# Job end times of the side work, POOL's DMA queue for the gate stores, and a third product from the old raw buffer

## The chip, the core and the metric

The kernel runs on one core of a Trainium2 chip. A core has five engines that each work through their own queue in a fixed order: PE (matrix products, results in PSUM), DVE (elementwise), ACT (elementwise, activation functions), POOL (elementwise, and it can issue DMAs), SP (issues DMAs only). They meet through semaphores. The metric is the device time of one execution in microseconds (us); the number compared is the median over several executions.

## What is computed

One layer of a decoder with 1024 prompt rows and 8 decode rows (1032 rows by 2048 columns). Cut to what matters:

```python
h = rmsnorm(x)
(aq, ak, av, iq, ik, iw, az, mq, mk, mv, mi, mf, mo, mz) = split(h @ w_in)
att = sparse_attend(top 256 keys of an index score)         # prompt; decode rows over a paged cache
h_ml, C, n, m = mlstm_run(mq, mk, mv, ig, lf)               # chunks, state C carried from chunk to chunk
a   = att * silu(az)
mo_ = rmsnorm_per_head(h_ml) * ml_norm_w * sigmoid(mo) * silu(mz)
x   = x + concat([a, mo_]) @ w_out
y   = rmsnorm(x)
```

The outputs are y for prompt and decode rows, the new keys and values and index keys, and the mLSTM states.

## The kernel before, in words

**The products.** Every fp32 operand of a large product is kept as a rounded high part H and a remainder L (`xH`, `xL`, `wH`, `wL`), and a product is the sum of three matmuls, H by H, H by L, L by H. Weights come by DMA into a raw fp32 buffer, ACT casts them to H, DVE subtracts to get L.

**Tiles.** The input projection is written as tiles numbered 0 to 60, and this number is also the clock by which side work is planned. Tiles up to 36 are plain (`mm`, L1500; `vproj`, L1569): T_MV = 9, T_AK = 17, T_AQ = 21, T_MQ = 29, T_MK = 33. From T_G = 37 to 60 comes the gate stage (`gate_stage`, matmuls L1729): the 24 tiles of the gates mo, mz and az as 12 pairs, each pair as 7 products of sums (kinds 0 to 4, 6, 7) in place of 8. That is 84 products of 48 matmuls with 258 columns, 4032 matmuls; after each half of a product `tick` is called, 168 "units" in all, each counted as one seventh of a tile. The products run in this order: kinds 4 and 6 together (units 0 to 47), kind 1 (to 71), kind 3 (to 95), kind 2 (to 119), and kinds 0 and 7 together (120 to 167). The sums of X rows that they multiply with are made early by the job `prep` (L1389 and around, DVE, ACT, POOL) and kept in DRAM as `xsD`; the sums of weights by the job `usum` (POOL DMAs that accumulate, L1419).

After the gate stage comes the output product for the last 264 rows (L1995, weights by `wsplit`, L248 to L252), then the tall product for the other 768 rows (L2056).

**Side work.** Attention, index scores, mLSTM and the preparations are written as generators ("jobs") in three lanes. A lane takes its jobs one after the other; at each tick `Lane.step` runs the current job until its share of work is done. The share follows from the job's weight and from the tile at which it is planned to end:

```python
quarters = max(1.0, self.job.end * 4 - self.now)
cost = w * quarters / max(self.left, w)
```

So a job's end sets how thickly its steps are written between the products. Lane 0 holds gates, index, att (prompt attention) and ml (prompt mLSTM); lane 1 prep, dscore, dsel, datt and dml (decode); lane 2 usum. What is written down this way is then given to a scheduler which fixes the order of every engine at build time; it can move an instruction forward or back, but not past what it depends on, and a buffer of a pool goes to its users in the order in which they were written.

**Prompt mLSTM.** `job_ml` has 16 steps, 8 chunks by 2 pairs of heads. One step is two transposes and two products for the scores (L853, L855), splits on ACT and DVE (`split`, L825 on ACT, L826 on DVE), then for each of two heads the matmuls of the output (L892) and of the state update (L896), then DVE, ACT and POOL, then transposes (L926). The products with qH, qL need the state C that an earlier step left, and buffers `dH`, `qH`, `CH`, `ksH` exist once each.

**PSUM.** The pool behind `bank()` has five banks; attention, mLSTM and decode jobs share them. The plain tiles and the gate stage have three more, `pj`. The last loop of the gate stage (kinds 0 and 7) needs four banks, so it takes one from `bank()`: `both = (pj[:2], [pj[2], bank()[:, :CS]])`. This bank can first be written when its earlier owners, written before unit 120, have been read.

**Gate weights.** `wide` (L1711 DMA, L1712 ACT cast, L1713 DVE) fetches the weights of a product into a raw buffer. The first products use the old raw buffer of the plain tiles (`one`, of which there is one: `wraw`); at a certain turn of the counter `turn["n"]` the rings of the plain tiles' wH and wL are turned into raw buffers, which the plain tiles must have left by then.

**Gate values.** In the last phases `gate_mz` and `gate_az` make two tanh operations on ACT, then two multiplications on POOL (`times`, L1790 and L1791 for az), then store 128 by 516 values to `gateS` in DRAM (L1782, L1792). The store was kept in the list `after` and issued on SP one product later. When the store of row k has been issued, `ready` gets k, and from tile T_PRE on `tick` issues `mixload` (L1468 the gate row from `gateS`, L1472 the attention or mLSTM row), and two ticks or more later `mixmake` (DVE L1477 and L1478, ACT, DVE), for the 14 rows of `PRE`; before the first of these the jobs ml and dml are run to their end.

Of the kernel before, what the change touches and what calls it, by code (L numbers as in the profile page):

```python
# [54 lines left out]
T_PRE = 58  # L55
# [115 lines left out]
def body(tc, A, stop=None):  # L171
# [1264 lines left out]
    def ix_weight(blocks):  # L1436
# [8 lines left out]
                   Job("att", T_MQ, 46.75, 2 * 2 * sum(2 * (1 + (i + 1) * 0.5) for i in range(8)) + 14, job_att, att_free),  # L1445
                   Job("ml", T_G + 9, T_PRE - 0.5, 38, job_ml)]),
             Lane([Job("prep", 4, T_AK, 8 * 16, job_prep),
                   Job("dscore", T_AK, 23, 24 + 128 + 2, job_dscore),
# [6 lines left out]
    after = []  # L1455
# [180 lines left out]
    def gate_stage():  # L1636
# [62 lines left out]
        def wide(kind, i):  # L1699
            turn["n"] += 1  # L1700
            if turn["n"] == 3:
                H, L = (wst.plain(name) for name in ("wH", "wL"))
                mlc["bc"] = raws[0][:2]
                raws[:] = [[x[:, 0], x[:, 1], x[:, 0:2]] for x in (H, L)] + [[H[:, 2], L[:, 2], None]]
                turn["raw"] = 0
# [69 lines left out]
        def gate_mz(j, h, e, g):  # L1775
            s2 = ev()
            half_tanh(s2, e)

            def times():
                G.tensor_tensor(s2, s2, e, OP.mult)  # L1780
                G.tensor_tensor(s2, s2, g, OP.mult)
            return times, lambda: SY.dma_start(row(8 + j)[:, cut(h)], flat(s2))  # L1782

        def gate_az(j, h, e, g):
# [7 lines left out]
            return times, lambda: SY.dma_start(row(j)[:, cut(h)], flat(s2))  # L1792

        def gate_raw(j):
            e, g = (take("s2", free).rearrange("p (c t) -> p c t", c=2) for _ in range(2))
            SY.dma_start(flat(e), row(j)[:, cut(0)])
            SY.dma_start(flat(g), rcS[j // 4][j % 4, :HR].partition_broadcast(128))
            push(*gate_az(j, 0, e, g))
# [66 lines left out]
        for i in range(NP):  # L1865
# [4 lines left out]
            with tc.high_priority():  # L1870
                for f in gate(i, 0, 1, combine(ps, got.pop(0), OP.add), g) or ():
                    f()
# [19 lines left out]
        def push(times, store, ks=()):  # L1892
            muls.append(times)
            after.append(lambda: (store(), ready.extend(ks)))

        def flush(n=1):
            while muls:
                muls.pop(0)()
            while len(after) > n:
                after.pop(0)()  # L1900

        for p, (z, i, y) in enumerate(order):
# [3 lines left out]
            with tc.high_priority():  # L1906
                fs = gate(i, 1, 1 - z, combine(both[y], e, OP.subtract, ev() if p > 1 else e), g)
            ks = () if z else [8 + i] if i < NM else [k for k in (2 * (i - NM), 2 * (i - NM) + 1) if k in PRE]
            push(*fs, ks)
# [17 lines left out]
    for f in after:  # L1927
        f()
# [436 lines left out]
```

## Time and profile before

| | |
|---|---|
| median of 3 executions | 2066.09 us (2060.03 to 2069.18) |
| the profiled execution, its own time | 2060.7 us |
| its span in the profile | 2058.6 us, 36195 instructions |
| mean granted clock of PE | 0.979 |
| PE busy | 1951.6 us, 12710 matmuls |
| DVE, ACT, POOL busy | 1436.4, 939.4, 417.0 us |
| DMA | 442.46 MB |
| gate stage | its first matmul starts at 946.4 us, its last at 1703.9 |
| mLSTM steps on PE | from 1421.3 to 1627.4 us |
| output product | its first matmul starts at 1704.0 us |

The profiled execution is one of its own; 2.1 us of its time lie outside the span. In the rows, L is a line of the kernel; "PEclk" is the granted clock of PE as a share of full speed; in a row of the timeline the bracket at the end gives how long the engine was idle before this instruction and what it waited for, "bank L892 <- ACT qH L825" in the waits means that matmuls of L892 into a tile named bank waited for ACT writing qH at L825.

### The profile page before, as it was taken

What the parts mean: (1) busy time and instruction counts of PE and PEld (TensorE: products, weight loads), DVE (VectorE), ACT (ScalarE), POOL (GpSimd) and SP (SyncE); (2) the same over time, 40 slices, a digit from 0 to 9 for tenths busy, and PEclk for the clock granted to TensorE, in tenths of its full rate; (3) what the DMA queues carried; (4) which work ended last, traced back from release to release, by engine and by line L of the source; (5) the groups of instructions that cost most, each with busy time, mean ns of one, the idle gap of its engine ahead of it and who ended that gap; (6) DMA issues with size and microseconds to landing.
All of it is one profiled execution on the core that took longest, in us unless ns stands there. A gap on an engine that the chain in (4) does not pass through costs nothing. (4 is left out here: it accounts for less than half of the span.)

```text
span 2058.6 us, 36195 instructions
## 1 busy us (share of the span) xinstructions
PE 1951.6 (95%) x12710; PEld 1841.5 (89%) x12710; DVE 1436.4 (70%) x3234; ACT 939.4 (46%) x1952; POOL 417.0 (20%) x420
## 2 busy tenths in 40 slices
PE   9988899999999999998999999999959998999997
PEld 9987788899999999998989999999959998986886
DVE  8454678976766677786835556666867575789886
ACT  8133455455313335321324555555656544455554
POOL 0111111213321010102210000000525452106542
PEclk9999999999999999999999999999979999999999
DMA  7567656667877587638645658677957877898875
GB/s 251 141 178 233 202 174 188 186 212 233 223 216 181 146 210 200 164 87 286 211 148 190 222 175 277 188 244 248 320 173 221 204 228 241 270 339 273 283 247 183
DMA packets 279603, 442.46 MB, mean 215 GB/s; under 512 B 41253, under 2 KB 142949, under 8 KB 275581
## 3 DMA queue, kind: packets, MB, share of 16 engines
q1 hardware_dynamic: 270189, 400.63, 61.0%
q0 software_dynamic: 7936, 37.76, 8.3%
q8 instruction: 100, 1.64, 0.3%
q10 hardware_dynamic: 1296, 1.77, 0.2%
q14 instruction: 82, 0.67, 0.1%
HBM read 344.33 MB, written 146.05 MB: 238 GB/s over the span
## 5 line engine op out<-in xcount | busy, mean ns | idle before, releaser
L1500 PE MATMUL pj<-xH,wH 128*128 128x344 f32 (+1 forms) x1200 | 389.3, 327 | 9.5 <-DVE iqe L377 5.1
L1500 PE MATMUL pj<-xL,wH 128*128 128x344 f32 (+1 forms) x1200 | 389.7, 325 | 0.0
L1500 PE MATMUL pj<-xH,wL 128*128 128x344 f32 (+1 forms) x1200 | 388.5, 324 | 0.0
L1729 PE MATMUL pj<-xH 128*128 128x258 f32 x1152 | 331.3, 288 | 9.6 <-DVE ev L1814 4.8
L1729 PE MATMUL pj<-xH,xL 128*128 128x258 f32 x1152 | 330.2, 287 | 2.5 <-DVE xL L1713 2.5
L1729 PE MATMUL pj<-xL,xH 128*128 128x258 f32 x1152 | 329.2, 286 | 0.9 <-issue 0.8
L1500 PEld LDWEIGHTS pj<-xH,wH 128*128 128x128 f32 x1200 | 226.6, 189 | 12.7 <-DVE iqe L377 6.1
L1729 PEld LDWEIGHTS pj<-xH 128*128 128x128 f32 x1152 | 220.0, 191 | 11.7 <-issue 4.6
L1500 PEld LDWEIGHTS pj<-xL,wH 128*128 128x128 f32 x1200 | 226.6, 189 | 1.3 <-DVE xL L309 0.3
L1500 PEld LDWEIGHTS pj<-xH,wL 128*128 128x128 f32 x1200 | 226.8, 189 | 0.9
L1729 PEld LDWEIGHTS pj<-xH,xL 128*128 128x128 f32 x1152 | 220.0, 191 | 5.2 <-DVE xL L1713 2.8
L1729 PEld LDWEIGHTS pj<-xL,xH 128*128 128x128 f32 x1152 | 220.2, 191 | 3.3 <-issue 2.3
L251 ACT CAST wH<-wraw 128x512 fp32r<-128x512 f32 (+2 forms) x183 | 109.7, 609 | 236.0 <-PE pj L1500 163.3
L252 DVE TENSOR_TENSOR wL<-wraw,wH 128x512 fp32r<-128x512 f32 (+2 forms) x183 | 129.7, 720 | 88.4 <-ACT wH L251 86.3
L2056 PE MATMUL pj<-wH,sH 128*128 128x512 f32 x336 | 132.4, 395 | 1.0 <-ACT wH L2040 0.8
L538 ACT ACTIVATE eq<-eq 128x512 bf16<-128x512 bf16 (+2 forms) x93 | 78.5, 844 | 117.1 <-DVE eq L537 107.8
L2056 PE MATMUL pj<-wH,sL 128*128 128x512 f32 x336 | 131.9, 393 | 0.0
L2056 PE MATMUL pj<-wL,sH 128*128 128x512 f32 x336 | 126.2, 394 | 4.0 <-DVE wL L2045 3.8
L491 ACT ACTIVATE rl<-bank 128x512 f32<-128x512 f32 (+2 forms) x160 | 79.8, 524 | 81.4 <-PE bank L489 47.3
L494 DVE SCALAR_TENSOR_TENSOR s<-rl,wiN,s 128x512 f32<-128x512 f32 (+2 forms) x150 | 98.8, 684 | 14.3 <-ACT rl L491 11.3
L489 PE MATMUL bank<-ki,qi 128*128 128x512 f32 (+2 forms) x320 | 79.1, 366 | 11.0 <-DMA qi<-qS 5.6
L882 POOL CAST aH<-onec 128x4 fp32r<-128x4 f32 x16 | 5.0, 314 | 375.0 <-DMA ev<-spD 375.0
(499 smaller groups left out, 4768.8 us busy)
## 6 DMA issues: line engine op xcount, KB each, us to landing
wraw<-in_wt_dram SPq DMA_DIRECT2D x144, 256.0 KB
wraw<-in_wa_dram SPq DMA_DIRECT2D x110, 256.0 KB
usD<-in_wa_dram POOLq DMA_DIRECT2D x48, 512.0 KB
xsD<-hl SPq DMA_DIRECT2D x80, 258.0 KB
wraw<-in_wo_dram SPq DMA_DIRECT2D x64, 256.0 KB
gateS<-ev SPq DMA_DIRECT2D x52, 258.0 KB
usD<-in_wa_dram SPq DMA_DIRECT2D x24, 512.0 KB
usD<-usD SPq DMA_DIRECT2D x24, 512.0 KB
```

The costliest lines, as they stand in the source:

```text
L251: a = SC.copy(H[:, s, :cols], raw[:, s, :cols])
L252: return a, V.tensor_tensor(L[:, s, :cols], raw[:, s, :cols], H[:, s, :cols].bitcast(F32), OP.subtract)
L489: PE.matmul(p[:, :cn], qi[:, h % 4, :], ki[x][:, c0:c0 + cn], start=(x == 0), stop=(x == 1))
L491: SC.activation(r[:, :cn], p[:, :cn], AF.Relu)
L494: v = V.scalar_tensor_tensor(s[:, c0:c0 + cn], r[:, :cn], wv, s[:, c0:c0 + cn], OP.mult, OP.add)
L538: SC.activation(junk2[:, :W1], junk2[:, :W1], AF.Copy, accum_out=cnt[:, 1:2])
L882: G.tensor_copy(aH[:, :, 256:258], onec)
L1500: m = PE.matmul(ps[:cols, :cn], w_[:, k, :cols], x_[kk][:, c0:c0 + cn], start=(kk == ends[0] and z == 0), stop=(kk == ends[1] and z == 2))
L1729: PE.matmul(ps[c], w_[:, q, ks], x[y][:, c * CS:c * CS + CS], start=(first and q == 0 and k == 0 and z == 0), stop=(q == 1 and k == 3 and ...
L2056: PE.matmul(ps[b], S_[x][:, b * 128:b * 128 + 128], T_[y], start=(k == 0 and z == 0), stop=(k == 7 and z == 2))
```

## The change

Five edits:

1. Planned ends: att from tile 46.75 to T_G + 13.5 = 50.5, ml from 57.5 to 58.25 (T_PRE - 0.25, where T_PRE itself goes from 58 to 58.5, which in units of the gate stage is from 147 to 151).
2. prep ends at T_AK + 1.5 = 18.5 in place of 17, dscore, the job behind it, at 24 in place of 23.
3. The rings of wH and wL become raw buffers at the fourth product in place of the third, so the third product's weights too come through `wraw`.
4. The stores of `gate_mz` and `gate_az` are issued by POOL, directly behind its two multiplications, and no longer by SP. There are 32 of them.
5. With that the list `after` goes; a row is `ready` when its multiplications and store have been written.

```diff
@@ -52,7 +52,7 @@
 T_G = 37
 T_AZ = 53
 NT = 61
-T_PRE = 58
+T_PRE = 58.5
 HR = R // 2
 CS = HR // 2
 NP = (NT - T_G) // 2
@@ -1442,17 +1442,16 @@
 
     lanes = [Lane([Job("gates", 5, T_MV - 0.5, 8500, job_gates),
                    Job("index", T_MV, 34.5, 3000 + sum(map(ix_weight, groups)), lambda: job_index(groups)),
-                   Job("att", T_MQ, 46.75, 2 * 2 * sum(2 * (1 + (i + 1) * 0.5) for i in range(8)) + 14, job_att, att_free),
-                   Job("ml", T_G + 9, T_PRE - 0.5, 38, job_ml)]),
-             Lane([Job("prep", 4, T_AK, 8 * 16, job_prep),
-                   Job("dscore", T_AK, 23, 24 + 128 + 2, job_dscore),
+                   Job("att", T_MQ, T_G + 13.5, 2 * 2 * sum(2 * (1 + (i + 1) * 0.5) for i in range(8)) + 14, job_att, att_free),
+                   Job("ml", T_G + 9, T_PRE - 0.25, 38, job_ml)]),
+             Lane([Job("prep", 4, T_AK + 1.5, 8 * 16, job_prep),
+                   Job("dscore", T_AK, 24, 24 + 128 + 2, job_dscore),
                    Job("dsel", T_MV, 33.5, 2000 + 31 * 1700 + 10000 + 16 * 2800 + 2000, job_dsel),
                    Job("datt", T_MQ, T_G + 4, 7500 + 8 * 5000 + 22000 + 5 * 4500 + 12000 + 16000 + 5000, job_datt, ix_free),
                    Job("dml", T_G, T_G + 13, 28000 + 16 * 2500 + 5000, job_dml, dml_free)]),
              Lane([Job("usum", T_AK + 1, T_G - 3, 8 * NP, job_usum)])]
     gateV = gateS.rearrange("(k p) r -> k p r", p=128)
     mixb = [None] * KT
-    after = []
 
     mctx = ExitStack()
     pb0 = None
@@ -1698,7 +1697,7 @@
 
         def wide(kind, i):
             turn["n"] += 1
-            if turn["n"] == 3:
+            if turn["n"] == 4:
                 H, L = (wst.plain(name) for name in ("wH", "wL"))
                 mlc["bc"] = raws[0][:2]
                 raws[:] = [[x[:, 0], x[:, 1], x[:, 0:2]] for x in (H, L)] + [[H[:, 2], L[:, 2], None]]
@@ -1779,7 +1778,8 @@
             def times():
                 G.tensor_tensor(s2, s2, e, OP.mult)
                 G.tensor_tensor(s2, s2, g, OP.mult)
-            return times, lambda: SY.dma_start(row(8 + j)[:, cut(h)], flat(s2))
+                G.dma_start(row(8 + j)[:, cut(h)], flat(s2))
+            return times
 
         def gate_az(j, h, e, g):
             s2 = ev()
@@ -1789,13 +1789,14 @@
             def times():
                 G.tensor_tensor(s2, s2, e, OP.mult)
                 G.tensor_tensor(flat(s2)[:, :n], flat(s2)[:, :n], flat(g)[:, :n], OP.mult)
-            return times, lambda: SY.dma_start(row(j)[:, cut(h)], flat(s2))
+                G.dma_start(row(j)[:, cut(h)], flat(s2))
+            return times
 
         def gate_raw(j):
             e, g = (take("s2", free).rearrange("p (c t) -> p c t", c=2) for _ in range(2))
             SY.dma_start(flat(e), row(j)[:, cut(0)])
             SY.dma_start(flat(g), rcS[j // 4][j % 4, :HR].partition_broadcast(128))
-            push(*gate_az(j, 0, e, g))
+            push(gate_az(j, 0, e, g))
 
         def gate(i, x, h, e, g=None):
             if i < NM and x == 0:
@@ -1868,7 +1869,8 @@
             ps, g = two(), factor(i, 0, 1)
             product(2, i, 2, ps, True, asker(2, i + 1))
             with tc.high_priority():
-                for f in gate(i, 0, 1, combine(ps, got.pop(0), OP.add), g) or ():
+                f = gate(i, 0, 1, combine(ps, got.pop(0), OP.add), g)
+                if f:
                     f()
         for j in late:
             todo += [None, None, None, lambda j=j: gate_raw(j)]
@@ -1889,24 +1891,23 @@
 
         for p in range(3):
             fetch(p)
-        def push(times, store, ks=()):
-            muls.append(times)
-            after.append(lambda: (store(), ready.extend(ks)))
-
-        def flush(n=1):
+        def push(times, ks=()):
+            muls.append((times, ks))
+
+        def flush():
             while muls:
-                muls.pop(0)()
-            while len(after) > n:
-                after.pop(0)()
+                times, ks = muls.pop(0)
+                times()
+                ready.extend(ks)
 
         for p, (z, i, y) in enumerate(order):
             fetch(p + 3)
             product(7 if z else 0, i, 0 if z else 1, both[y], not z, flush)
             e, g = fetched.pop(p)
             with tc.high_priority():
-                fs = gate(i, 1, 1 - z, combine(both[y], e, OP.subtract, ev() if p > 1 else e), g)
+                f = gate(i, 1, 1 - z, combine(both[y], e, OP.subtract, ev() if p > 1 else e), g)
             ks = () if z else [8 + i] if i < NM else [k for k in (2 * (i - NM), 2 * (i - NM) + 1) if k in PRE]
-            push(*fs, ks)
+            push(f, ks)
         flush()
 
     vproj()
@@ -1924,8 +1925,6 @@
     wst.open()
     with tc.high_priority():
         first = [wsplit(A["wo"][0, q], 128, wst, 2, 3) for q in range(3)]
-    for f in after:
-        f()
     while mids:
         mixmake(*mids.pop(0))
     xctx.close()
```

Lines between 1450 and 1780 have numbers lower by one in the changed kernel (L1729 becomes L1728, L1711 L1710, L1468 L1467, L1472 L1471); the store L1792 of before is L1792 there too, on POOL.

**PE, mLSTM steps within the gate stage.** Before, PE's queue in the middle of a run of seven steps (`CH`, `CL` the split state, `qH`, `qL` the split queries, `aH`, `aL` the values, `dH`, `dL` the decayed scores):

```order
L892 MATMUL bank<-CH,qL 128x258
L892 MATMUL bank<-aH,dH 128x258
L892 MATMUL bank<-aL,dH 128x258
L892 MATMUL bank<-aH,dL 128x258
L853 MATMUL bank<-qkv 128x128 x2
L855 MATMUL bank<-cst,qkv 128x128 x2
L892 MATMUL bank<-CH,qH 128x258
L892 MATMUL bank<-CL,qH 128x258
L896 MATMUL bank<-aH,ksH 128x258
```

After, PE's queue at the end of the step that stands at the same place of the gate stage, ahead of the first matmul into the extra bank:

```order
L892 MATMUL bank<-aH,dL 128x258
L896 MATMUL bank<-aH,ksH 128x258
L896 MATMUL bank<-aL,ksH 128x258
L896 MATMUL bank<-aH,ksL 128x258
L926 MATMUL bank<-cst,hm 128x128 x4
L853 MATMUL bank<-qkv 128x128 x2
L855 MATMUL bank<-cst,qkv 128x128 x2
L1728 MATMUL bank<-xH 128x258
L1728 MATMUL bank<-xL,xH 128x258
L1728 MATMUL bank<-xH,xL 128x258
```

Before, a step's last product is followed by the next step with no matmul of the gate stage between; after, gate matmuls (L1728) follow. Counted over the whole queue, the number of gate matmuls (of 4032) that have gone by when a step begins its products is, before, 2786, 2850, 2939, 3000, seven times 3024, 3071, 3141, 3223, 3296, 3371; after, 2745, 2785, 2873, 2939, 2999, 3024, 3072, 3120, 3228, 3323, 3421, 3490, 3562, 3628, 3703, 3773. (Matmul 3025 is the first into the extra bank, in both.)

**SP, the loads for the first products of the gate stage.** Before, SP's queue up to the load of the third product's weights, which goes to `wH` (`xsD` holds the sums of X rows; `mlS` takes the mLSTM's queries and keys):

```order
L1671 DMA xH<-xsD 128x516
L419 DMA mlS<-ev 128x2x128
L424 DMA mlS<-ev 128x88
L424 DMA mlS<-ev 128x40
L419 DMA mlS<-ev 128x2x128
L1711 DMA wH<-in_wa_dram 128x2x512
L1716 DMA wH<-in_wa_dram 128x512
L1711 DMA wL<-in_wa_dram 128x2x512
```

After, from the second to the third product's load and on:

```order
L1710 DMA wraw<-in_wa_dram 128x2x512
L1670 DMA xL<-xsD 128x516
L1670 DMA xH<-xsD 128x516 x2
L1670 DMA xL<-xsD 128x516
L1670 DMA xH<-xsD 128x516
L1710 DMA wraw<-in_wa_dram 128x2x512
L1670 DMA xL<-xsD 128x516
L1670 DMA xH<-xsD 128x516
L1155 DMA slotS<-rai 128x16
L419 DMA mlS<-ev 128x2x128
```

The third product's load now goes to `wraw`, five loads behind the second's and ahead of the last stores of the plain tiles (L419, L424); the first load to `wH` is the fourth product's, and stands behind them as before.

**SP, the end of the gate stage.** Before, SP's queue as the gate stage ends (`wraw` from `in_wo_dram` is the output product's weights, `mL`, `mH` the rows of the mix):

```order
L1792 DMA gateS<-ev 128x516 x2
L248 DMA wraw<-in_wo_dram 128x512 x2
L1792 DMA gateS<-ev 128x516
L1468 DMA mL_18359<-gateS 128x264
L248 DMA wraw<-in_wo_dram 128x512
L1468 DMA mL_18398<-gateS 128x264
L1792 DMA gateS<-ev 128x516 x2
L248 DMA wraw<-in_wo_dram 128x512 x5
```

After:

```order
L1467 DMA mL_18299<-gateS 128x264
L1471 DMA mH_18298<-attS_108 128x264
L1467 DMA mL_18338<-gateS 128x264
L1471 DMA mH_18337<-attS_108 128x264
L248 DMA wraw<-in_wo_dram 128x512 x6
L1467 DMA mL_18479<-gateS 128x264
```

The stores L1792 are no longer on SP, and six weight loads stand together behind the loads of the mix. On PE's side the 14 early loads of the mix lay between gate matmuls 3558 and 3976 before, and lie between 3891 and 4016 now.

**DVE, the front.** Edit 2 moves the splits of `prep` (L1389, `hl`) on DVE's queue. Counted between the evacuations of the plain tiles 5 to 8 (L377, `iqe`, two a tile), 4, 2, 5 and 10 of them stand ahead of a tile's first evacuation before, and 4, 8, 2 and 5 after; the others come later, beside the tiles that follow.

## The prediction

> **What bounds the kernel now.** I read the page first: its first line, the busy time of each engine, and PE's two rows of forty slices.
>
> ```profile
> span 2058.6 us, 36195 instructions
> PE 1951.6 (95%) x12710; PEld 1841.5 (89%) x12710; DVE 1436.4 (70%) x3234; ACT 939.4 (46%) x1952; POOL 417.0 (20%) x420
> PE   9988899999999999998999999999959998999997
> PEclk9999999999999999999999999999979999999999
> ```
>
> PE is busy 1951.6 of 2058.6 us, so 107 us of idle time is all that a better order can win, and what PE does at less than full clock. One slice (the 30th, about 1493 to 1544 us) stands out in both rows: busy 5 tenths, clock 7 tenths. The waits of PE, grouped by what was waited for (engine, waiting line, releaser: us in total, times, longest), say which stalls are large:
>
> ```profile
> PE bank L892 <- ACT qH L825: 27.1, 8, 5.2
> PE bank L1995 <- ACT wH L251: 5.6, 1, 5.6
> PE pj L1569 <- DVE iqe L377: 5.6, 1, 5.6
> PE pj L1500 <- DVE iqe L377: 5.1, 2, 3.5
> PE pj L1729 <- DVE ev L1814: 4.8, 5, 1.5
> PE pj L1729 <- ACT xH L1712: 3.5, 1, 3.5
> PE pj L1729 <- DVE xL L1713: 2.5, 1, 2.5
> ```
>
> The five edits aim at four of these places: the mLSTM's matmuls (L892), the third product's weights (L1712, L1713), the boundary to the output product (L1995, L251) and the evacuations at the front (L377). Then the windows (length; busy time of PE, PEld, DVE, ACT, POOL, each with its count; PE's granted clock; DMA share; GB/s), for these places and, as a yardstick, for a stretch in which PE never stops:
>
> ```profile
> 947.00:972.00 25.00, 18.86 (x128) 18.35 (x129) 17.81 (x22) 3.24 (x4) 6.18 (x7) 0.80 1.05 354
> 1493.00:1550.00 57.00, 32.53 (x169) 30.95 (x170) 36.34 (x109) 32.94 (x88) 15.28 (x34) 0.70 0.56 168
> 1553.00:1628.00 75.00, 70.26 (x582) 69.22 (x581) 56.86 (x129) 48.14 (x110) 44.72 (x51) 1.00 0.82 227
> 1700.00:1720.00 20.00, 14.40 (x103) 13.96 (x103) 9.30 (x16) 7.39 (x13) 6.19 (x5) 0.83 0.53 176
> 1720.00:1770.00 50.00, 50.00 (x412) 50.00 (x411) 35.13 (x57) 25.32 (x50) 6.73 (x8) 1.00 0.87 280
> 1421.00:1720.00 299.00, 257.99 (x1997) 253.22 (x1998) 209.11 (x509) 165.20 (x365) 126.58 (x143) 0.93 0.78 233
> ```
>
> The yardstick: 412 matmuls in 50.00 us, 0.121 us each, at clock 1.00 (the upper of PE's two levels, 2.4 GHz). A stretch with n matmuls is worth n x 0.121; what it is longer is lost. By that the stretch from 1493 to 1550 is worth 169 x 0.121 = 20.5 us and takes 57: **36.5 us lost**. From 947 to 972 it is 128 x 0.121 = 15.4 of 25: **9.6 lost**. From 1700 to 1720, 103 x 0.121 = 12.5 of 20: **7.5 lost**.
>
> **Edit 1, the planned ends.** PE's timeline shows what the lost 36.5 us are made of (start, duration, line, and in brackets PE's idle time and its releaser), here the first and the last of six steps and two later ones; the second fence is the window's row for the gate stage's own matmuls alone (PE, PEld).
>
> ```profile
> 1496.08 0.39 PE L892 MATMUL bank<-CH,qH 128*128 128x258 f32 x1 [3.41 <-ACT qH L825]
> ...
> 1545.27 0.58 PE L892 MATMUL bank<-CH,qH 128*128 128x258 f32 x1 [3.35 <-ACT qH L825]
> ...
> 1585.99 0.39 PE L892 MATMUL bank<-CH,qL 128*128 128x258 f32 x1 [1.48 <-DVE qL L826]
> 1599.78 0.39 PE L892 MATMUL bank<-CH,qH 128*128 128x258 f32 x1 [1.86 <-ACT qH L825]
> ```
>
> ```profile
> 1493.00:1550.00 57.00, 0.00 (x0) 0.00 (x0) 0.70 0.56 168
> ```
>
> From 1493 to 1550 PE runs no gate matmul: seven mLSTM steps stand in a row. Six of them begin from 1496.08 to 1545.27, so one comes every 49.2 / 5 = 9.84 us. That is the length of the chain through ACT, DVE and POOL; PE's own part is 169 / 5.8 = 29 matmuls or 3.5 us, and PE waits for the rest. The granted clock of the stretch is 0.70, part of it at the lower level of 1.2 GHz. The reason for the run is the bank: gate matmul 3025 is the first into the bank taken from `bank()`, and that bank's earlier owners are mLSTM tiles, written ahead of it in the program because ml was planned to be 11 steps along by unit 120. In the new order six steps stand ahead of it, the sixth after a gap of 25 gate matmuls and the others 40 to 88 apart; behind it the steps go on at 48, 48 and 108.
>
> What is left to pay: a gap of g gate matmuls gives g x 0.121 us of work beside the step's own 3.5 us, against a chain of 9.84. The new short gaps are 25, (40), 48 and 48: waits of 3.3, 1.5, 0.5 and 0.5, together 5.8. For the rest the stretch from 1553 to 1628 is the price: steps 47 to 82 gate matmuls apart, and 75 - 582 x 0.121 = 4.6 us lost over five steps, 0.9 each. Three more of the former seven at 0.9 are 2.7. So 8.5 of the 36.5 us remain: **-28**. Bounds: nothing remains, -36.5; or all seven pay the longest wait of the spaced steps, 1.86, beside the 5.8: 19 remain, -17.5. I take the middle row because the new gaps are for the most part like those of 1553 to 1628. That att now ends at 50.5 costs nothing that I can see: the first mLSTM step of both orders stands at nearly the same gate matmul (2786, now 2745), so attention held PE's mLSTM up to there already and the plan only catches up with it.
>
> **Edit 3, the third product.** Its rows, on SP, DVE, ACT and PE:
>
> ```profile
> 938.68 0.54 SPq L1711 DMA_DIRECT2D wraw<-in_wa_dram  x1
> 954.99 0.38 SPq L1711 DMA_DIRECT2D wH<-in_wa_dram  x1
> ```
>
> ```profile
> 945.83 1.23 DVE L1713 TENSOR_TENSOR xL<-wraw,xH 128x1024 fp32r<-128x1024 f32 x1 [0.22 <-issue]
> ```
>
> ```profile
> 961.07 1.04 ACT L1712 CAST xH<-wH 128x1024 fp32r<-128x1024 f32 x1 [15.28 <-DMA wH<-in_wa_dram]
> ```
>
> ```profile
> 962.16 0.58 PE L1729 MATMUL pj<-xH 128*128 128x258 f32 x1 [3.53 <-ACT xH L1712]
> 965.90 0.58 PE L1729 MATMUL pj<-xH,xL 128*128 128x258 f32 x1 [2.51 <-DVE xL L1713]
> ```
>
> The third load was issued at 954.99, on SP behind the last stores of the plain tiles, and its data was cast 6.1 us later. `wraw` is free when the second product's split ends, 945.83 + 1.23 = 947.1. The load can go then and is cast at 947.1 + 6.1 = 953.2 and split by about 955.5, while PE has work to 958.6 (962.16 - 3.53). So the waits of 3.53 and 2.51 and part of the lower clock (0.80) go: **-7**, between 0 (the DMA engines show a share of 1.05 in this stretch, so a load may only take another's place, and the fourth product's load, still behind the stores, can be the late one) and -9.6. What moves behind it: five loads of `xsD` and stores L419, L424 are one load later on SP; the next reader of those is half a product away.
>
> **Edits 4 and 5, the gate stores and the boundary.**
>
> ```profile
> 1700.31 7.18 SPq L1792 DMA_DIRECT2D gateS<-ev  x2
> ```
>
> ```profile
> 1707.72 4.11 SPq L248 DMA_DIRECT2D wraw<-in_wo_dram  x5
> ```
>
> ```profile
> 1705.84 1.31 POOL L1791 TENSOR_TENSOR ev<-ev,xL 128x516 f32<-128x516 f32 x1
> ```
>
> ```profile
> L1468 SPq DMA_DIRECT2D mL<-gateS x16: 319/424/500, 1648.0 to 1713.9; - x16
> ```
>
> ```profile
> L1419 POOL DMA_DIRECT2D usD<-in_wa_dram x48: 766/994/1806, 465.0 to 946.4; - x48
> ```
>
> SP stood 7.18 us at two stores until POOL's last products were done (1705.84 + 1.31), and only then issued five weight loads of the output product; PE's wait of 5.6 for `wH` follows from that. Now SP has no store there, so these loads go earlier, which could bring the whole 7.5 us back. But the 14 early rows of the mix, each two loads, have moved from gate matmuls 3558 to 3976 into 3891 to 4016 and stand ahead of the six weight loads: 28 issues of 0.42 us (the median of the 16 rows of L1468) are 12 us of SP in the last 17 us of the stage. I take **-2**, between -7.5 and +8 (nine or ten of those rows, two loads of 0.42 us each, on the path).
>
> On POOL the 32 stores cost 32 x 0.99 = 32 us at the median of POOL's only DMAs in this trace (L1419), up to 58 at their longest. POOL is busy 126.6 of the 299 us in which they fall, and 44.7 of 75 in the densest part, so they fit: **0**, at most +5 where a multiplication waits behind a store and holds one of the four `ev` buffers. It isn't below nothing, since what SP gains is counted at the boundary. The Trainium skill, page "DMA: Bandwidth & Descriptors", section "SWDGE vs HWDGE vs iDMA", speaks against this edit: a plain transfer belongs on SP or ACT, and only accumulating, casting or irregular ones on GpSimd, whose cores build each descriptor in software. The trace agrees as to the price on POOL (0.99 us for L1419, whose loads accumulate). By that rule the term would lie toward its +5; by the rows it is 0, because POOL has the room.
>
> **Edit 2, the front.** DVE splits `hl` in bursts ahead of an evacuation for which PE waits:
>
> ```profile
> 181.74 0.43 DVE L1389 TENSOR_TENSOR hl<-X,hl 128x258 fp32r<-128x258 f32 x1 [0.65 <-ACT hl L1388]
> ...
> 188.55 0.43 DVE L1389 TENSOR_TENSOR hl<-X,hl 128x258 fp32r<-128x258 f32 x1 [1.04 <-ACT hl L1388]
> 188.90 0.55 DVE L377 TENSOR_TENSOR iqe<-pj,rstd 128x388 f32<-128x388 f32 x1
> ```
>
> Five of them, from 181.74 to 188.55, take 1.4 us or so each, with ACT between; then comes the evacuation, and PE had waited 5.6 us. All such waits together are 5.6 + 5.1 = 10.7 us. In the new order the last group falls from 10 splits to 5, the group two tiles earlier grows from 2 to 8: the first halves 5.6, the second adds six splits of 1.4 to a wait of 3.5, part of which PE has in hand as it has elsewhere (10 splits gave 5.6, so about 0.56 each, +3.4). Together +0.6, and later tiles get the splits that moved on, one or two each: **+2**, between -5 (the last group's wait gone) and +9 (all six splits at 1.4 exposed). dscore a tile later costs nothing: no wait in the list above is its own, and dsel, which follows it in the lane, keeps its end.
>
> **The sum.** -28 - 7 - 2 + 0 + 2 = -35. The profiled execution took 2060.7 (its span and 2.1 us): 2060.7 - 35 = 2025.7. The median of the runs shown, 2066.1, stands 5.4 above it, the lowest 0.7 below; I add 3 for where a median of three will lie: **2029 us**. The terms' ends, taken as independent, give -14 and +18: 2015 to 2047.
>
> **Rivals.**
>
> *The steps still wait.* Steps that are farther apart keep half their waits, since ACT and DVE are at work for the gate stage between them and the chain itself becomes longer than 9.84. For: 27.1 us over 8 waits is only the visible part, and the gap of 25 is there. Against: 1553 to 1628. Then -14 in place of -28: 2043. Chance 0.08.
>
> *POOL's stores come late.* A late store keeps its `ev` buffer, the evacuation L1814 that wants it waits, and PE with it. For: L1419 shows 0.77 to 1.81 us for one kind of issue. Against: POOL's 126.6 of 299 us. If each of the last 24 products waited as long as L1814's longest wait, 1.5 us, that is 36: 2065. The Trainium skill, page "SBUF — State Buffer", warns of this under "SBUF: two separate sides" (a DMA of GpSimd starves while DVE holds the port pair that they share). Chance 0.05.
>
> *The mix is late (the slower side).* Before, the 16 gate rows were loaded over 66 us (1648.0 to 1713.9), 56 of them under the gate stage; now the first starts 141 gate matmuls, 17 us, before its end. If they need the same 66 us, 49 are exposed: 2060.7 + 3 - 33 (the sum without the boundary) + 49 = 2080. It decides where the output product's first matmul waits for `mH` or `mL`. Against: the pace was set by when the gate values came; now most of them lie ready when the first load goes. Chance 0.04.
>
> *It doesn't do what it says.* The bank taken from `bank()` is held by another late owner, and the wait stays under another name: -7 alone, and 2057. Against: six steps ahead of matmul 3025 in place of eleven. Chance 0.05.
>
> **How the numbers follow.** What a measurement of this kernel can tell from no change is about 0.5%, 10.3 us: faster is under 2055.8, slower over 2076.4. The forecast has 0.78, the first rival 0.08, both faster: 0.86. The second and the fourth are within: 0.10. The third is slower: 0.04. The range takes the forecast's 2015 to 2047, the first rival, and at the top most of the way to the fourth; at the bottom the terms' better ends if two of them come together (-36.5 and -9.6 in place of -28 and -7 are another 11): 2010 to 2054.
>
> **What would show it.** Right: no slice of PE at 5 tenths and none at clock 7 between 1421 and 1720; L892 behind ACT qH under 12 us in all; no wait at the third product; the output product's first weights without a wait of 5; POOL at some 450 us busy. Wrong: L892's waits spread over more steps with the same sum; waits of L1814 over 10 us; the first matmuls of the output product waiting for `mH` or `mL`; a larger sum behind `iqe`.

## The result, and the profile after

The changed kernel takes 2034.19 us (median of four, 2024.72 to 2038.85) against 2063.57 for the kernel before, measured beside it: a ratio of 0.9849, 95% interval 0.9805 to 0.9894. In a second measurement, with the kernel before measured anew beside it, the ratio was 0.9848 (0.9830 to 0.9866). The forecast was 2029, in 2010 to 2054. The profiled execution took 2036.12 us, its span is 2034.3.

The first rows of the page after, and PE's two rows of slices:

```profile
span 2034.3 us, 36236 instructions
PE 1946.6 (96%) x12710; PEld 1837.0 (90%) x12710; DVE 1434.5 (71%) x3234; ACT 939.1 (46%) x1952; POOL 434.4 (21%) x452
...
PE   9989999998999999999999999999988997999998
PEclk9999999999999999999999999999999998999999
```

The slice that stood at 5 tenths is gone; the lowest is now the 34th, about 1678 to 1729 us, right behind the gate stage's end, and the clock's only 8 is there too. PE's waits over the whole span, after (engine, waiting line, releaser: us in total, times, longest):

```profile
PE bank L1994 <- ACT wH L251: 8.9, 2, 6.3
PE bank L892 <- ACT qH L825: 7.5, 4, 3.1
PE pj L1499 <- DVE iqe L377: 6.3, 3, 4.0
...
PE pj L1728 <- DVE ev L1815: 3.9, 2, 2.4
...
PE bank L892 <- DVE qL L826: 2.6, 3, 1.2
```

L892's wait for `qH` fell from 27.1 to 7.5, the third product's two waits are no longer in the list, and the wait for the output product's weights grew from 5.6 to 8.9. Windows of the profile after (length; busy PE, PEld, DVE, ACT, POOL; PE's clock; DMA share; GB/s), beside the three of before:

```profile
947.00:972.00 25.00, 25.00 (x209) 24.93 (x208) 10.09 (x31) 6.67 (x8) 7.02 (x7) 1.00 0.92 285
...
1493.00:1550.00 57.00, 48.64 (x348) 47.58 (x349) 39.62 (x84) 34.38 (x76) 33.79 (x42) 0.88 0.71 227
1553.00:1628.00 75.00, 72.59 (x609) 72.12 (x608) 59.66 (x133) 48.11 (x110) 43.89 (x59) 1.00 0.79 243
...
1673.00:1700.00 27.00, 15.19 (x83) 13.04 (x82) 17.48 (x34) 11.16 (x23) 7.14 (x7) 0.68 0.62 196
```

At 0.121 us a matmul the stretch from 1493 to 1550 now loses 57 - 348 x 0.121 = 14.9 us where it lost 36.5; the first 25 us of the gate stage lose nothing. But the 27 us behind the gate stage's end lose 27 - 83 x 0.121 = 17.0. Where stages begin and end is read from the last start of each line's matmuls, of which these are the gate stage, the output product and the tall product after, and the output product before:

```profile
L1728 PE MATMUL bank<-xH,xL x192: 277/282/419, 955.0 to 1672.8; 128*128 128x258 f32 x192
```

```profile
L1994 PE MATMUL bank<-mH,wL x256: 280/285/590, 1673.1 to 1783.8; 128*128 128x264 f32 x128
```

```profile
L2055 PE MATMUL pj<-wL,sH x336: 388/389/504, 1784.4 to 2024.9; 128*128 128x512 f32 x168
```

```profile
L1995 PE MATMUL bank<-mH,wL x256: 278/284/588, 1704.3 to 1805.5; 128*128 128x264 f32 x128
```

The same rows of every kernel give this table (us, one profiled execution each; "tail" is from the last tall matmul to the end of the span). Executions of one kernel differ by up to some 10 us: the changed kernel's two profiles have 725.5 and 715.0 for the gate stage. The times in the table are for finding a place; what an edit is worth is told by the ratios, each from the medians of several executions.

| kernel | plain tiles to | gate stage | output product | tall product | tail | ratio to before (95%) |
|---|---|---|---|---|---|---|
| before | 946.2 | 757.7 | 101.6 | 240.4 | 12.7 | 1 |
| changed | 947.3 | 725.5 | 111.0 | 241.1 | 9.4 | 0.9849 (0.9805 to 0.9894) |
| changed, again | 945.3 | 715.0 | 110.5 | 239.3 | 9.9 | 0.9848 (0.9830 to 0.9866) |
| att's end alone | 941.1 | 718.3 | 107.7 | 240.8 | 12.8 | 0.9895 (0.9869 to 0.9921) |
| edit 1 alone | 942.0 | 722.3 | 107.0 | 241.6 | 12.8 | 0.9886 (0.9865 to 0.9908) |
| all but edit 1 | 943.0 | 768.3 | 105.1 | 244.7 | 10.9 | 1.0070 (1.0047 to 1.0092) |
| all but edits 4, 5 | 939.4 | 720.7 | 111.9 | 240.0 | 12.8 | 0.9882 (0.9856 to 0.9907) |
| bank taken early | 939.6 | 720.8 | 110.6 | 239.7 | 12.8 | 0.9897 (0.9867 to 0.9928) |
| att's end, POOL | 942.4 | 729.7 | 108.7 | 240.9 | 9.6 | 0.9902 (0.9868 to 0.9937) |
| att's end, third load | 944.6 | 725.5 | 103.3 | 240.0 | 12.8 | 0.9877 (0.9849 to 0.9905) |
| edit 2 alone | 937.0 | 756.6 | 104.1 | 240.1 | 12.8 | 1.0007 (0.9989 to 1.0026) |
| edits 4, 5 alone | 936.8 | 756.6 | 104.3 | 240.1 | 9.3 | 1.0016 (0.9998 to 1.0035) |
| edit 3 alone | 944.8 | 764.1 | 105.1 | 239.2 | 12.7 | 1.0049 (1.0030 to 1.0068) |
| att's end, third load, bank early | 941.4 | 718.3 | 110.1 | 240.5 | 12.8 | 0.9896 (0.9868 to 0.9923) |

Before to after: +1.1 up to the gate stage, -32.2 in it, +9.4 in the output product, +0.7 in the tall product, -3.3 in the tail, together -24.3.

### The profile page after: what moved, and what is told of

Same layout as the page of the kernel before. It is cut to its first block, busy times and chain, and to the rows that moved or that the text cites. A ratio compares the mean times of both kernels' runs of the same rounds, so it can differ in the third digit from the quotient of the medians.

```text
span 2034.3 us, 36236 instructions
## 1 busy us (share of the span) xinstructions
PE 1946.6 (96%) x12710; PEld 1837.0 (90%) x12710; DVE 1434.5 (71%) x3234; ACT 939.1 (46%) x1952; POOL 434.4 (21%) x452
## 5 line engine op out<-in xcount | busy, mean ns | idle before, releaser
L1728 PE MATMUL pj<-xH 128*128 128x258 f32 x1152 | 330.8, 287 | 6.6 <-DVE ev L1815 3.9
L1728 PE MATMUL pj<-xL,xH 128*128 128x258 f32 x1152 | 330.8, 287 | 1.1 <-issue 1.1
L1728 PE MATMUL pj<-xH,xL 128*128 128x258 f32 x1152 | 330.5, 287 | 1.4 <-issue 1.3
L1728 PEld LDWEIGHTS pj<-xH 128*128 128x128 f32 x1152 | 220.2, 191 | 9.8 <-issue 4.3
L1728 PEld LDWEIGHTS pj<-xH,xL 128*128 128x128 f32 x1152 | 220.2, 191 | 3.7 <-issue 3.1
L1728 PEld LDWEIGHTS pj<-xL,xH 128*128 128x128 f32 x1152 | 220.1, 191 | 2.2 <-issue 1.3
L494 DVE SCALAR_TENSOR_TENSOR s<-rl,wiN,s 128x512 f32<-128x512 f32 (+2 forms) x150 | 101.6, 700 | 13.5 <-ACT rl L491 10.4
L1994 PE MATMUL bank<-mH,wH 128*128 128x264 f32 x256 | 74.3, 292 | 10.6 <-ACT wH L251 8.9
```

The source lines that it names most:

```text
L494: v = V.scalar_tensor_tensor(s[:, c0:c0 + cn], r[:, :cn], wv, s[:, c0:c0 + cn], OP.mult, OP.add)
L1728: PE.matmul(ps[c], w_[:, q, ks], x[y][:, c * CS:c * CS + CS], start=(first and q == 0 and k == 0 and z == 0), stop=(q == 1 and k == 3 and ...
L1994: PE.matmul(p, w_[:, k, :], x_, start=(n == 0), stop=(n == 47))
```

## The experiments

The theory was that the gain is the spacing of the mLSTM steps (edit 1), and that the run of steps without a gate matmul between them came from the turn of the extra bank. The first rival was that the gain came from SP, freed of the gate stores.

**Att's end alone.**

```diff
-                   Job("att", T_MQ, 46.75, ...
+                   Job("att", T_MQ, T_G + 13.5, ...
```

> The kernel before with one number changed: att ends at T_G + 13.5 in place of 46.75 (ml, T_PRE, the stores and the loads as before). Theory A (the gain is the spacing of the mLSTM steps, and the end of att sets it; in this build's order on PE the sixteen steps stand 51 to 84 gate matmuls apart with no run at matmul 3025): L892's wait for ACT qH is under 8 us, no slice of PE below 8 tenths between 1421 and 1720, and the stage gains about 28; the boundary to the output product stays as before (about 7.5 us lost) because the mix loads stay where they were: about 2063.6 - 28 = 2036, +-8. Theory B (the gain came from SP, which no longer stands at the gate stores): no gain, 2058 to 2066.

Measured 0.9895. The gate stage fell by 39 us (in a profiled execution that is 11 us below this kernel's median), and L892's wait for `qH` is nearly gone; the row of its waits and the window in which the run stood:

```profile
PE bank L892 <- ACT qH L825: 2.1, 3, 1.0
```

```profile
1493.00:1550.00 57.00, 51.68 (x420) 50.19 (x420) 48.19 (x97) 37.22 (x84) 38.93 (x41) 1.00 0.86 280
```

One number brings two thirds of the gain (1.05 of 1.5%), with the stores still on SP: the rival falls. What was expected of the boundary fell too: the output product took 107.7, not 101.6.

**Edit 1 alone**: the same, with `T_PRE = 58.5` and ml's end at `T_PRE - 0.25`.

> The kernel before with edit 1 whole (att's end, ml's end and T_PRE), nothing else. Theory A: the steps are spaced as with att's end alone, so the stage gains about 28; if the 9 us that the output product lost in the changed kernel come from the later mix loads (T_PRE 58.5), they show here too and the kernel is 5 to 10 us slower than with att's end alone: about 2043, +-8. If they come from the POOL stores, it is equal to att's end alone: 2036. Theory B: 2058 to 2066.

Measured 0.9886, and 107.0 us for the output product: equal to att's end alone. So the later T_PRE and ml's end cost nothing there, and bring nothing that these runs can tell. The stretch in which the run stood:

```profile
1493.00:1550.00 57.00, 53.20 (x437) 52.08 (x436) 47.37 (x95) 37.89 (x86) 41.40 (x44) 1.00 0.91 291
```

It loses 57 - 437 x 0.121 = 4.1 us here, where the changed kernel loses 14.9.

**All but edit 1**: the changed kernel with

```diff
-T_PRE = 58.5
+T_PRE = 58
-                   Job("att", T_MQ, T_G + 13.5, ...
-                   Job("ml", T_G + 9, T_PRE - 0.25, 38, job_ml)]),
+                   Job("att", T_MQ, 46.75, ...
+                   Job("ml", T_G + 9, T_PRE - 0.5, 38, job_ml)]),
```

> The changed kernel with edit 1 undone (att 46.75, T_PRE 58, ml T_PRE - 0.5); the third load, the POOL stores and prep stay changed. Theory A: the run is back (in this build's order eight steps stand at gate matmul 3024), L892's wait for ACT qH is 25 us or more; only the third product's 7 us are left: about 2057, +-8. Theory B: most of the gain stays: about 2040.

Measured 1.0070, slower than the kernel before. The run is back:

```profile
PE bank L892 <- ACT qH L825: 29.0, 8, 4.8
```

The theory's direction holds, its size does not: the other edits were expected to keep 7 us and lose 15 instead.

**All but edits 4 and 5**: the changed kernel with the gate stores and the list `after` as before (the stores on SP).

```diff
-                G.dma_start(row(j)[:, cut(h)], flat(s2))
-            return times
+            return times, lambda: SY.dma_start(row(j)[:, cut(h)], flat(s2))
```

> The changed kernel with edits 4 and 5 undone: the gate stores are on SP again, one product later. Theory A: the spacing of the steps is nearly that of the changed kernel, POOL's stores were worth nothing: 2034, +-6, and if the mix loads' crowd is what costs the output product its 9 us, that loss stays. Theory B: 2050 or more. If the POOL stores caused the loss at the output product: about 2025.

Measured 0.9882; the output product takes 111.9 us with the stores on SP as well. POOL's stores are not the loss there, and of the gain they are at most a small part: the changed kernel has 0.9849 and 0.9848, with intervals that overlap this one.

**The bank taken early**, in the kernel before, all plans untouched:

```diff
+        xb = bank()[:, :CS]
+        V.memset(xb, 0.0)
         fill(0, 4)
         ask(2, 0)
...
-        both = (pj[:2], [pj[2], bank()[:, :CS]])
+        both = (pj[:2], [pj[2], xb])
```

> The kernel before with the extra bank of the last loop taken and first written (one memset of 128 by 258 on DVE, whose values the first product overwrites) ahead of the kind 2 loop, at unit 96, where six mLSTM steps are written, not at unit 122 behind eleven; all plans as before. In this build's order the steps stand 60 to 84 gate matmuls apart, with no run, the last at 3883. Theory A1 (the run of seven comes from the bank's turn): L892's wait for ACT qH is under 10 us and the gate stage is 20 to 30 us shorter than before's 757.7; the mix comes later than in any other kernel, so the output product is 5 to 12 us longer than before's 101.6; together 15 to 20 under the kernel before. Theory A2 (the run only shows that att's early end crowds ACT and DVE; spaced steps would wait as well): L892's waits stay over 20 us in sum, and the time within 5 us of before.

Measured 0.9897, the gate stage 720.8. L892's wait for `qH` is one of 0.8 us:

```profile
PE bank L892 <- ACT qH L825: 0.8, 1, 0.8
```

```profile
1493.00:1550.00 57.00, 52.31 (x414) 51.89 (x414) 46.69 (x93) 35.99 (x81) 37.55 (x39) 0.94 0.85 262
```

This tells the cause: with att still planned to end at 46.75, moving only the point at which the bank is taken and first written spaces the steps and gives what att's end gives. Taking and first write moved together here, so the run does not tell which of the two counts.

**Att's end and POOL's stores.** Diff: that of att's end and edits 4 and 5.

> The kernel before with att's end at T_G + 13.5 and the gate stores on POOL, nothing else. With att's end alone the output product took 107.7 us, and SP issued its second group of weight loads 6.7 us after the last gate matmul, behind two gate stores. Theory S (those stores are what is late): without them the group goes before or at the end of the gate stage, the output product takes 98 to 102 us, and the kernel is 6 to 9 us faster than with att's end alone: ratio to before near 0.985. Theory D (behind the stores the weight buffers themselves are late, since DVE's splits stand behind the mix): the group goes 5 to 13 us after the end as in the changed kernel, and the time equals att's end alone, ratio near 0.989.

Measured 0.9902, as with att's end alone (0.9895), the output product 108.7. Theory S falls. SP's second group of weight loads, with no store ahead of it, and what SP waited for around it:

```profile
1679.42 4.61 SPq L248 DMA_DIRECT2D wraw<-in_wo_dram  x5
```

```profile
SPq L248 <- DVE wL L252: 19.9, 7, 9.1
```

The group goes 7.3 us after the last gate matmul (1672.1), because DVE's splits, which free the raw buffers, are late.

**Att's end and the third load.** Diff: that of att's end, and `turn["n"] == 4`.

> The kernel before with att's end at T_G + 13.5 and the third product's weights through the old raw buffer, nothing else. Theory A: the third product's waits (4.7 us for ACT xH in the run with att's end alone) go, -5 to -8 against att's end alone: ratio near 0.986. Rival: another load takes the DMA engines' time and the wait goes to the fourth product: ratio near 0.989, with a wait of 3 us or more at L1729 within 972 to 1000 us.

Measured 0.9877 against 0.9895 for att's end alone: the intervals overlap, and 2.6 us of the wait for `xH` at L1712 are left. Inconclusive in time; what removes these waits is seen in edit 2 alone and edit 3 alone, below.

**Edit 2 alone.**

```diff
-             Lane([Job("prep", 4, T_AK, 8 * 16, job_prep),
-                   Job("dscore", T_AK, 23, 24 + 128 + 2, job_dscore),
+             Lane([Job("prep", 4, T_AK + 1.5, 8 * 16, job_prep),
+                   Job("dscore", T_AK, 24, 24 + 128 + 2, job_dscore),
```

> The kernel before with edit 2 alone (prep to T_AK + 1.5, dscore to 24). In this build's order the mLSTM starts its first step at gate matmul 2871 in place of 2786, and eight steps stand in a row at 3024. Theory A (these edits make the run longer unless att's end moves): L892's wait for ACT qH is 28 us or more, the kernel 5 to 12 us slower than before: ratio near 1.004. Rival (the front gains what it was made for): the waits for iqe fall by 5 us and the kernel is as fast as before or faster: ratio 0.997 to 1.0.

Measured 1.0007, no difference, where 1.004 was expected. The run is dearer (L892 waits 29.4 us), and PE's waits for `iqe` fell from 10.7 to 5.0 us. Above all, the start of the gate stage runs without a stop, with the third load still at the old turn. Its first 26 us in this kernel, in the kernel before and in edit 3 alone (below):

```profile
937.20:963.20 26.00, 26.00 (x219) 26.00 (x219) 13.27 (x34) 6.28 (x8) 7.77 (x9) 1.00 0.94 298
```

```profile
946.40:972.40 26.00, 19.64 (x135) 18.92 (x135) 18.41 (x22) 3.24 (x4) 6.78 (x8) 0.80 1.04 353
```

```profile
945.00:971.00 26.00, 21.11 (x157) 20.58 (x157) 18.54 (x24) 4.98 (x6) 6.45 (x7) 0.87 1.03 350
```

219 matmuls with edit 2, 135 before, 157 with edit 3; the DMA share is 0.94 with edit 2 in place of 1.04. What has moved are the loads of the decode attention (`datt`, a later job of the lane of prep and dscore): gathers of `ck` issued by POOL, and on SP the loads of `qb`. The gathers with edit 2, and before:

```profile
L1279 POOL DMA_INDIRECT ck<-in_ck_dram,idxs x16: 951/957/1692, 948.8 to 991.2; - x16
```

```profile
L1279 POOL DMA_INDIRECT ck<-in_ck_dram,idxs x16: 947/950/1702, 938.7 to 989.2; - x16
```

Before, the first gather goes 7.7 us ahead of the gate stage's first matmul (946.4), and at the third product's load SP stands 3.5 us, which the profile puts down to `qb` landing; that load is issued 8.6 us after the first matmul. With edit 2 the third load is issued at 937.53, 0.3 us after the first matmul, and its data is cast 5.0 us later; the first gather comes after that, 11.6 us behind the first matmul. So it is in all profiles: the five with edit 2 have the first gather 11 to 14 us behind the stage's first matmul and no wait of PE for the third product's weights, the nine without it have the gather some 8 us ahead and such a wait. That it is these loads is read from this order; no run moved the decode attention alone.

**The changed kernel again.** No edit.

> The changed kernel once more, so that the other three stand beside it on one chip. Ratio to the kernel before 0.981 to 0.989, as first measured.

Measured 0.9848.

**Att's end, third load and the bank taken early.** Diff: the three together.

> The kernel before with att's end at T_G + 13.5, the third load through the old raw buffer, and the extra bank taken and first written at unit 96 (the memset). In this build's order the steps stand 68 to 92 gate matmuls apart, from 2632 to 3768. If the bank's turn and att's end are two ways to remove one and the same run, little is left for the bank to bring: L892's waits under 3 us, ratio 0.985 to 0.989, within 0.3% of the changed kernel. If they add up (each shortens the mLSTM on its own), ratio 0.982 or less, faster than the changed kernel by over 0.3%.

Measured 0.9896: no better than either way alone (L892 waits 6.7 us, the output product takes 110.1), and outside both ranges that were expected (0.985 to 0.989, and 0.982 or less). The two do not add up; they remove one and the same run. No kernel tried here beats the changed one.

**Edits 4 and 5 alone.** Diff: as the change has them.

> The kernel before with edits 4 and 5 alone (gate stores on POOL). In this build's order six mLSTM steps stand in a row at 3024 in place of seven (counted with the one that ends the spaced ones). Theory A: POOL has room for 32 issues of 0.6 us, the run stays: L892's wait for ACT qH 20 to 28 us, ratio 0.996 to 1.003. Rival: POOL's stores are what made the changed kernel without edit 1 0.7% slower than before: ratio 1.004 or more.

Measured 1.0016 (0.9998 to 1.0035): POOL has the room, and the run stays (L892 waits 26.7 us). The stores of L1792 on POOL, after, and on SP, before (ns: least, median, most):

```profile
L1792 POOL DMA_DIRECT2D gateS<-ev x16: 580/615/674, 1445.9 to 1688.8; - x16
```

```profile
L1792 SPq DMA_DIRECT2D gateS<-ev x16: 319/352/606, 1451.6 to 1711.9; - x16
```

**Edit 3 alone.**

```diff
-            if turn["n"] == 3:
+            if turn["n"] == 4:
```

> The kernel before with edit 3 alone (the third product's weights through the old raw buffer). In this build's order the first mLSTM step stands at 2833 in place of 2786 and a run of seven at 3024 stays. Theory A: the waits at the third product (6 us) go and the run stays: ratio 0.995 to 0.999. Rival: the shift makes the run dearer and eats the gain: ratio 1.001 or more.

Measured 1.0049: slower. PE's two waits at the third product in this kernel:

```profile
959.58 0.58 PE L1729 MATMUL pj<-xH 128*128 128x258 f32 x1 [2.89 <-ACT xH L1712]
962.81 0.58 PE L1729 MATMUL pj<-xH,xL 128*128 128x258 f32 x1 [2.00 <-DVE xL L1713]
```

Of 6.0 us 4.9 are left. The third load and its cast on ACT:

```profile
946.52 0.38 SPq L1711 DMA_DIRECT2D wraw<-in_wa_dram  x1
```

```profile
958.48 1.05 ACT L1712 CAST xH<-wraw 128x1024 fp32r<-128x1024 f32 x1 [14.62 <-DMA wraw<-in_wa_dram]
```

The load goes 8.5 us earlier than before (954.99), but its data is cast 12.0 us after the issue in place of 6.1. The mLSTM's run costs 2 us more (L892 waits 29.1 us in 9 times), and a wait of 4.6 us for the cast of another product's weights (L1712) has come up at about 1655 us; why is not known. Alone, edits 2, 3 and 4 with 5 add 0.07, 0.49 and 0.16%, together 0.72%; all but edit 1 measured 0.70%. Two of the three are not clear of nothing, so that the sum fits may be chance.

## Why the prediction was right, and where its steps were not

**Edit 1, -28: the mechanism right, the size too large.** The run was the bank's turn (the bank taken early shows it), and it went. The gate stage became 32.2 us shorter, of which (218 - 135) x 0.121 = 10.0 belong to its first 26 us, so 22 are left for the mLSTM. The new short gaps were expected to leave 8.5; the waits did come to 7.5 + 2.6 = 10.1, but the granted clock of the stretch was 0.88, so 14.9 us were lost there. The short gaps are not edit 1's own: with edit 1 alone the steps' products begin 59 to 84 gate matmuls apart from the third step on and the stretch loses 4.1 us, while with edits 1 to 3 the gaps of 48 are there and it loses 57 - 374 x 0.121 = 11.7. Att's end and edit 3 together have gaps of 55 and 48 there and lose 57 - 405 x 0.121 = 8.0; what edit 2 does to them beside edit 1 was not run. One count ahead of the prediction is off: in the profile before, six steps and not seven begin their products (the first L892 of each) at gate matmul 3024, and the last step at 3447; a seventh has only its scores there. What was overlooked is how att's end works. I wrote that the plan "only catches up"; in the run with att's end alone the decode mLSTM's updates on DVE lie 100 us earlier. Their row before, and with att's end alone:

```profile
L1230 DVE SCALAR_TENSOR_TENSOR Cb<-wraw,dec,Cb x64: 326/346/1436, 1282.4 to 1467.7; 128x128 f32<-128x128 f32 x64
```

```profile
L1230 DVE SCALAR_TENSOR_TENSOR Cb<-wraw,dec,Cb x64: 340/345/352, 1182.8 to 1367.8; 128x128 f32<-128x128 f32 x64
```

Before, they ran into the first prompt steps (PE from 1421.3); with att's end alone they were over. The shorter gate stage doesn't need it: with the bank taken early they lie where they lay before, and the gate stage is as short:

```profile
L1230 DVE SCALAR_TENSOR_TENSOR Cb<-wraw,dec,Cb x64: 328/347/1443, 1275.1 to 1461.0; 128x128 f32<-128x128 f32 x64
```

What att's end does beside it is to leave fewer steps written ahead of the bank's first use (seven have begun their products ahead of gate matmul 3025 in that profile, ten before); that this alone does the work there is argued, not shown.

**Edit 3, -7: the size came by luck, the step failed.** The waits went, and the stage's first 26 us gained 10.0, but edit 2 took the waits away, not the old raw buffer: edit 2 alone has none of them, edit 3 alone keeps 4.9 of 6.0 us. The prediction let the cast follow the earlier issue by the same 6.1 us; with edit 3 alone it follows by 12.0, in a stretch in which the DMA engines show a share of 1.03. This is the bound of 0 that the prediction gave for just this reason.

**Edits 4 and 5 on POOL, 0: right.** The Trainium skill's rule (page "DMA: Bandwidth & Descriptors", section "SWDGE vs HWDGE vs iDMA": plain transfers belong on SP or ACT) was weighed against the room on POOL. The trace agrees that an issue costs more on POOL, 0.615 us against 0.352 on SP for the same store, and at 1.0016 for edits 4 and 5 alone this does not reach the time. The term was sized with 0.99 us an issue, from loads that accumulate; POOL's busy time grew by 17 us (417.0 to 434.4) and not by 32. The stall of which the Trainium skill warns (page "SBUF — State Buffer", section "SBUF: two separate sides") is not to be seen: the longest of these 16 issues is 0.674.

**The boundary, -2: failed, +9.4.** The freed SP was expected to bring the weight loads forward. They came later, 12.9 us after the last gate matmul (1672.8) in place of 3.8. What SP waited for, before and after (windows 1655:1735 and 1655:1700):

```profile
SPq L1792 <- POOL ev L1791: 19.7, 6, 6.5
```

```profile
SPq L248 <- DVE wL L252: 16.3, 5, 9.2
```

After, on SP, ACT, DVE and PE:

```profile
1685.70 4.63 SPq L248 DMA_DIRECT2D wraw<-in_wo_dram  x6
```

```profile
1683.81 0.63 ACT L1754 ACTIVATE ev<-ev 128x516 f32<-128x516 f32 x1 [0.88 <-DVE ev L1815]
1684.35 0.60 ACT L251 CAST wH<-wraw 128x512 fp32r<-128x512 f32 x1
```

```profile
1684.98 0.69 DVE L252 TENSOR_TENSOR wL<-wraw,wH 128x512 fp32r<-128x512 f32 x1 [1.26 <-ACT wH L251]
```

```profile
1693.24 0.59 PE L1994 MATMUL bank<-mH,wH 128*128 128x264 f32 x1 [6.26 <-ACT wH L251]
```

The raw buffer was free only when DVE had split it at 1684.98 + 0.69 = 1685.67; the cast ahead of that stood in ACT's queue behind a tanh (L1754) that waited for the last evacuation. That evacuation was late on DVE. Before, and after:

```profile
1704.23 0.43 DVE L1814 TENSOR_TENSOR ev<-bank,xH 128x258 f32<-128x258 f32 x1 [0.90 <-PE bank L1729]
```

```profile
1677.58 2.97 DVE L1476 SCALAR_TENSOR_TENSOR mx<-mL,mH 128x264 f32<-128x264 f32 x2 [0.17 <-DMA mH<-attS]
1680.47 0.99 DVE L1485 TENSOR_TENSOR mL<-mx,mH 128x264 fp32r<-128x264 f32 x2
...
1683.31 0.42 DVE L1815 TENSOR_TENSOR ev<-bank,xH 128x258 f32<-128x258 f32 x1
```

Before, it started 0.3 us after the last gate matmul; after, 10.5 us, because instructions of the mix stand ahead of it in DVE's queue, which was busy for 9.26 of the 10.14 us up to it. The stores were one of two things that were late, and with them gone the other took their place. The prediction looked at SP's issues for the mix and not at the mix's work on DVE. The slower rival had the right place (the mix work crowds the end) at a fifth of its price, and the sign "first weights without a wait of 5" failed (longest wait 6.3). That the later T_PRE is the reason was tried and falls: the output product took 107 to 108 us with T_PRE at 58 and at 58.5. It is longer than in the one profile of before in every other kernel of the table, 103.3 to 111.9, also where the gate stage got longer (105.1 twice), so some 3 us of the 9.4 need no shorter gate stage. Nor is the late evacuation all of it: with att's end and POOL's stores it starts 2.9 us behind the last gate matmul, and the output product still takes 108.7. What more weight buffers would give back is open; no run tried them.

**The front, +2**: +1.1, which is inside what plain tiles differ between kernels (936.8 to 947.3).

The sum of -35 against -24.3 in the profiled executions, and -29.4 between the medians: a gain that was too large by 6 in the mLSTM and too large by 11 at the boundary, with 3 to 4 each on the other side at the gate stage's start and in the tail. That the time lies so near the forecast is in part luck: the gain at the stage's start came by another edit than the one it was put down to, and the one in the tail was not foreseen. A slip of its own: the lower ends of its terms, taken as independent, give -12.6 and not -14.

What is left open is the last part of the gain. Edit 1 alone has 0.9886 and the changed kernel 0.9849 and 0.9848, and no run tells which of the other edits brings the difference: edits 2 and 3 beside edit 1 have 0.9882, POOL's stores beside att's end 0.9902.

## What to carry to other kernels

In this kernel a tile from a shared pool waited for the work whose instructions were written before its first use: take the tile, and write it, before the side work that shares the pool is thick, or plan that side work so that less of it is written ahead. Test an edit of a schedule alone and with the others: edit 3 here costs 0.5% by itself, and the stall that it was aimed at went by an edit made elsewhere. A queue freed of one wait shows the next: before counting on it, read when the buffer that its next instruction fills comes free.

## What the runs showed that was not expected

The tail, from the last tall matmul to the end of the span, is 12.7 or 12.8 us in the nine profiles of kernels that store the gate values from SP and 9.3 to 10.9 in the five of kernels that store them from POOL. The last issue on SP starts 4 to 5 us after the last tall matmul in both; the difference lies behind it, where the trace shows no instruction. Why is not known.
